# Two-layer streaming encoder on one core: mask copies, the ring of query parts, the quadrant sums, resting outputs and the last residual additions change their places

## The chip, the core and the metric

The kernel runs on one core of a Trainium2 chip. The metric is the device time of one execution in microseconds (us), the median over several runs. A core has five engines that run side by side, each in the order of its own queue: TensorE (PE: matrix products and transposes; the load of its weights is listed as PEld), VectorE (DVE), ScalarE (ACT), GpSimd (POOL) and SyncE (SP), which here only issues transfers. Transfers run on 16 DMA engines. Products are accumulated in banks of PSUM, and everything else lies in SBUF.

## The reference

What is computed are two transformer layers for 1024 prompt frames and 64 sample frames with shared weights, in float32:

```python
xp, xs = x_prompt, x_sample                      # (1, 1024, 1024), (1, 64, 1024)
for l in range(2):
    if l == 0:
        mp = _even_prompt(xp, ...)               # latent attention (8 heads) and chunk-band attention (8 heads)
        ms = _even_sample(xs, ...)
    else:
        mp = _odd_prompt(xp, ...)                # stick-breaking attention, 16 heads
        ms = _odd_sample(xs, ...)
    xp = _post_block(xp, mp, ...)
    xs = _post_block(xs, ms, ...)

def _even_project(x, pos, w_in, g_q, w_uq, g_kv):
    h = x @ w_in
    q_a = (_rms_norm(h[..., :768], g_q) @ w_uq).reshape(B, S, 8, 96)
    q_a = concat([q_a[..., :64], _rope(q_a[..., 64:], pos)])
    ckv = _rms_norm(h[..., 768:1024], g_kv)
    ...

def _post_block(x, mix, g1, b1, g2, b2, w_up, w_down):
    x = _layer_norm(ALPHA * x + mix, g1, b1)
    ff = jnp.square(jax.nn.relu(x @ w_up)) @ w_down      # 1024 -> 4096 -> 1024
    return _layer_norm(ALPHA * x + ff, g2, b2)
```

The outputs are the two results and the new cache rows of each attention.

## The kernel before

All products are done in split precision: a float32 operand is split into a rounded high part H and a remainder L (`split`, L152 on ScalarE and L153 on VectorE), and a product is three matmuls, H by H, H by L and L by H (`mm3`, L157 to L159). So an operand is ready for TensorE only when ScalarE and VectorE have both dealt with it.

The program is written with a tile framework that puts instructions into the queue of each engine in an order that a simulated timeline gives, and adds the waits. A tile's tag names a ring of buffers, and its count is the ring's length: the next tile of a tag waits until the oldest one is no longer read. `after(x, mark)` adds an order without a wait: x is put into its queue only once the instruction `mark` has its place in the timeline. All transfers are issued by SP, in its queue's order, on eight lanes; a transfer waits for the one eight before it.

**Latents and queries (layer 0).** `latents` goes over nine tiles of 128 tokens. First it makes the compressed keys (`cat`, stored to `o_lat`; `stgH`, `stgL` and `krT`, stored to `ck_d` and `krT_d`, L413 to L424). Then it makes the query latents: two products of 384 columns, squares with a sum on ScalarE (L445), a reciprocal root, the scaled `qn` on VectorE (L453), and its transposes on TensorE (L175), which are split into `qn0`, `qn384` and `qn768`. In this second loop, two copies of a constant mask `qconst` into the DRAM tensor `qr_d` are issued (L437), and two of the query weights are loaded and split (`weight`, L193).

`queries` multiplies the latents by six blocks of `w_uq`. Blocks 0 to 3 (`u0` to `u3`) are loaded and split there. Each result is split into H and L in a buffer `raw` (`parts`, L152 and L153) from which it is stored to `qm_d`, or for the rotated blocks by quarters to `qr_d` (L513). TensorE writes the products by turns into banks s and d.

**After the mixer, in both layers.** `out_proj` makes the output projection tile by tile, with a residual (L1186), the layer norm (statistics L296 and L298, `rv` L201, `neg` L302, on ScalarE L303, the scaling L304, the bias L305 on VectorE or GpSimd) and the transposes of the result (L175, from `xs` or `sl`), which are written to the four quadrants of each half c of the tokens. `quadrant_sums(c)` gives a list of closures that are called one by one: four that split a quadrant, then `sums` (four differences on VectorE, L271), then four that split the sums and the last quadrant. `up` multiplies by `w_up`: `plain(m, c)` does the first two blocks of columns in the plain way, `work(m)` does blocks 2 to 15 by a Strassen scheme with seven products that use the sums. The squared outputs go to the DRAM tensor `a_d` (`store`, L1305).

`down` multiplies by `w_down`. `strassen(q)` is called for q = 0 to 48, seven products for each of seven groups; each loads operands three products ahead (`load_a`, L1412; `load_w`), splits them one ahead (`ahead`) and adds the product to accumulators (L1488 on VectorE, L1492 on ScalarE for the first ones). In the last group the combined sums M1, U2 and W1 are added to each other, on GpSimd and VectorE (L1398, the helper `tt`). `finish` does the last group in the plain way: a product for each half of a row tile, added to `acc` (also `tt`, L1398), with W1 and the residual x22 added by L1599 and S0 by `tt`, and then the layer norm.

Big buffers come from a list of free slots (`Slots`): `take` gives the first free one that fits, `give` puts one at the end of the list. The slots are named `sl`, `xs`, `wo`, `wH`, `wL` and `wraw`; a slot that has been given back can be taken at once, and then its next writer waits until a transfer from it is done.

Of the kernel before, what the change touches and what calls it, by code (L numbers as in the profile page):

```python
# [13 lines left out]
P = 128  # L14
# [109 lines left out]
class Net:  # L124
# [116 lines left out]
    def quadrant_sums(self, c):  # L241

        sl = self.slots
        f = dict(enumerate(self.xq[c]))

        def sums():
            f.update({i: sl.take([4, TC]) for i in (4, 5, 6)})
            self.sums(*(f[i] for i in range(7)))  # L250
            for i in (0, 2, 3):
                sl.give(f[i])

        def part(i, give=False):
            if i in self.xqH[c]:
                sl.give(self.xqH[c][i])
                sl.give(self.xqL[c][i])
            H, L = (sl.take([4, TC], F32R) for _ in "HL")
            self.split(H, L, f[i])
            self.xqH[c][i], self.xqL[c][i] = H, L  # L260
            if give:
                sl.give(f[i])

        return [lambda i=i: part(i) for i in (0, 2, 1, 3)] + [sums] + [lambda i=i: part(i, True) for i in (5, 6, 4, 1)]
# [64 lines left out]
    def latents(self):  # L329
# [102 lines left out]
        for t, (t0, n) in enumerate(TOK):  # L432
            if t == 1:

                rows = io["qconst"].unsqueeze(0).to_broadcast([4, ROPE, 2, T])
                for r in (96, 0):
                    self.after(nc.sync.dma_start(self.qr_d[:, r : r + ROPE], rows), marks[-2])  # L437
# [29 lines left out]
    def queries(self, qn, uw):  # L467
# [4 lines left out]
        def load(m):  # L472
            if m < 4:
                raw = self.tl(up, [P, KQ, P], "uraw", 2)
                nc.sync.dma_start(raw, io["w_uq"][m])
                uw[m] = [self.tl(up, [P, KQ, P], f"u{m}{x}", 1, F32R) for x in "HL"]
                self.split(*uw[m], raw, mark=marks[-1])
# [4 lines left out]
        def nope(m, c):  # L482
            c0, n = CHUNKS[c]
            ps = self.ps("ds")
            uq(ps, m, c, n)
            nc.sync.dma_start(self.qm_d[m, :, :, c0 : c0 + n], self.parts(up, ps[:, :n], 4))

        def rotate(c):
# [21 lines left out]
            for i, r in enumerate((x1, x2)):  # L510
                x = self.parts(up, r, 4)
                for o, base in ((0, 64), (1, 32)):
                    nc.sync.dma_start(self.qr_d[:, base + 16 * i : base + 16 * i + 16, :, c0 : c0 + n], x[o * 64 : o * 64 + 64])  # L513
# [748 lines left out]
    def up(self, layer):  # L1262
# [6 lines left out]
        F, W = {}, {}  # L1269
        AHEAD, PLAIN = 3, 2  # L1270

        def load(m):
# [21 lines left out]
        def product(ps, w, XH, XL, first=True, last=True):  # L1294
            for k in range(4):
                self.mm3(ps, w[:, 0, k, :], w[:, 1, k, :], XH[:, k, :], XL[:, k, :], first and k == 0, last and k == 3)

        def store(m, c, out, A):
            s = slice(c * TC, c * TC + TC)
            if m < 14:  # L1300
# [3 lines left out]
                nc.sync.dma_start(self.a_d[m, 4:, :, s].rearrange("i p t -> p i t"), out[1])  # L1304
            nc.sync.dma_start(self.a_d[m, :4, :, s].rearrange("i p t -> p i t"), out[0])  # L1305
            for x in out:
                sl.give(x)

        def plain(m, c):

            out, A = outputs()
            XH, XL = self.xqH[c], self.xqL[c]
            for h in range(2):
                for half in range(2):
                    ps = self.bank()[:, :TC]
                    for j in range(2):
                        b = 2 * j + half
                        product(ps, W[m, 2 * h + j], XH[b], XL[b], j == 0, j == 1)
                    o = A[2 * half + h]
                    nc.scalar.activation(o, ps, AF.Relu)  # L1320
                    nc.scalar.activation(o, o, AF.Square)
                if c:
                    for j in range(2):
                        sl.give(W.pop((m, 2 * h + j)))
            store(m, c, out, A)

        def work(m, hook):
# [57 lines left out]
    def down(self, layer, xres, xout, last):  # L1385
# [9 lines left out]
        prods = ((0, 0), (1, 2), (5, 5), (6, 6), (3, 1), (4, 4), (2, 3))  # L1395
        NQ = 7 * (NG - 1)
        B, A8, A, W = {}, {}, {}, {}
        tt = lambda e, x, y: e.tensor_tensor(x, x, y, op=ALU.add)  # L1398
# [95 lines left out]
        def strassen(q):  # L1494
            gr, m = divmod(q, 7)
            f0, end = gr == 0, gr == NG - 2
            if not end:
                if m == 1:
# [20 lines left out]
            for i in range(4):  # L1519
# [7 lines left out]
                if end:  # L1527
# [10 lines left out]
                    elif m == 5:  # L1538
                        tt(p, U2[i], W1[i])
                        tt(p, W1[i], acc[i + 4][:, hi])  # L1540
                    elif m == 6:
                        tt(nc.vector, acc[i][:, hi], U2[i])
            if m in (0, 1, 5):
# [14 lines left out]
        def finish():  # L1558
# [19 lines left out]
            for t in order:  # L1578
                n = sum(r[1] for r in rows[t])
                for h in range(2):  # L1580
# [3 lines left out]
                    if n == P:  # L1584
                        r = slice(t % 4 * P, t % 4 * P + P)
                        for k in range(4):
                            aH, aL = la[2 * (t // 4) + k // 2]
                            self.mm3(ps, aH[:, k % 2, r], aL[:, k % 2, r], *mov[k], k == 0, k == 3)
                    else:
                        self.mm2(ps, [a8[:, k, :] for k in range(4)], mov)  # L1590
                    tt(nc.vector, acc[t][:, c], ps)
                    if n < P:
# [3 lines left out]
                        sl.give(tmp)  # L1596
                if t == order[0]:
                    for i in range(4):
                        nc.vector.scalar_tensor_tensor(acc[i + 4][:, hi], x22[0][i], ALPHA, W1[i], op0=ALU.mult, op1=ALU.add)  # L1599
                    for c in (lo, hi):  # L1600
                        tt(nc.vector, acc[8][:, c], S0)
                    if not last:
# [56 lines left out]
    def post(self, layer, ws, ys, side, xres, xmid, xout, last):  # L1659
# [36 lines left out]
        do(1, 4)  # L1696
        do(0, 2)
        plain(1, 0)
        load(2)
# [126 lines left out]
```

## Time and profile before

| | before |
|---|---|
| median of 3 runs | 2820.95 us (2818.41 to 2821.55) |
| the profiled execution | 2826.57 us, span 2824.8 us |
| mean granted clock of TensorE | 0.989 |
| busy: PE, PEld | 97%, 89% |
| busy: DVE, ACT, POOL | 76%, 54%, 27% |
| transfers | 331 MB, 117 GB/s |

The span runs from the first to the last instruction of one profiled execution; what lies around it is 1.8 us here. A list of waits names the waiting engine and line, what it waited for, the total in us, how often, and the longest. A row of a timeline has the start in us, the length, engine, line, operation and tiles, and in brackets the idle time before it with what ended it. A row of windows has the stretch, its length, for each of the five engines the busy time and the number of instructions, the granted clock (1.00 is full), the busy share of the DMA engines and GB/s. Buffer numbers are left out of names.

### The profile page before, as it was taken

How to read it: one execution, taken by the hardware profiler on the slowest of the kernel's cores; microseconds unless marked ns; L12 is line 12 of the kernel's file. 1: busy time of each engine (PE TensorE's matmuls, PEld its weight loads, DVE VectorE, ACT ScalarE, POOL GpSimd, SP SyncE). 2: the span in 40 equal slices, each digit the busy share in tenths (PEclk: the TensorE clock that was granted, in tenths of full speed). 3: DMA queues.
4: the chain of work that ended last, by engine and by line, in shares of the span. 5: the costliest groups of instructions: out<-in, count | busy, mean ns of one | idle time of the engine just before them, and what ended most of it. 6: DMA issues, size and time to landing. Idle time of an engine off the chain costs nothing. (4 is left out here: it accounts for less than half of the span.)

```text
span 2824.8 us, 46956 instructions
## 1 busy us (share of the span) xinstructions
PE 2737.9 (97%) x16931; PEld 2500.8 (89%) x16931; DVE 2158.5 (76%) x3833; ACT 1513.2 (54%) x3103; POOL 749.5 (27%) x879
## 2 busy tenths in 40 slices
PE   8999998999999999999999999999999999999998
PEld 7999997888899998788789999998789999977786
DVE  4346667885867777899977888878787777789998
ACT  4236666883555556333257777777545555543331
POOL 3022323652100002222543333434330000022245
PEclk9999999989999999999999999999999999999999
DMA  7142224434244457443421111112252443664432
GB/s 220 36 154 69 67 84 101 109 102 137 88 136 144 134 167 254 127 151 116 134 83 61 52 59 52 54 51 77 79 167 87 153 148 129 227 196 127 151 124 83
DMA packets 226800, 331.33 MB, mean 117 GB/s; under 512 B 44488, under 2 KB 159240, under 8 KB 226504
## 3 DMA queue, kind: packets, MB, share of 16 engines
q1 hardware_dynamic: 226568, 328.34, 36.8%
q8 instruction: 134, 2.20, 0.3%
q14 instruction: 98, 0.80, 0.1%
HBM read 216.58 MB, written 109.99 MB: 116 GB/s over the span
## 5 line engine op out<-in xcount | busy, mean ns | idle before, releaser
L723 POOL TENSOR_TENSOR G<-G,S 128x384 f32<-128x384 f32 (+4 forms) x200 | 200.6, 1007 | 346.3 <-DVE S L720 129.8
L157 PE MATMUL d<-xH,wH 128*128 128x384 f32 (+1 forms) x784 | 262.7, 335 | 3.1 <-ACT qS L608 2.3
L159 PE MATMUL d<-xH,wL 128*128 128x384 f32 (+1 forms) x784 | 261.6, 334 | 0.0
L158 PE MATMUL d<-xL,wH 128*128 128x384 f32 (+1 forms) x784 | 260.4, 332 | 0.0
L153 DVE TENSOR_TENSOR wtL<-t,wtH 128x512 fp32r<-128x512 f32 (+2 forms) x328 | 197.0, 618 | 47.1 <-ACT wtH L152 38.4
L152 ACT ACTIVATE wtH<-t 128x512 fp32r<-128x512 f32 (+2 forms) x328 | 170.3, 545 | 48.1 <-PE t L175 21.4
L1483 POOL MEMSET sl<- 64x1024 f32 x2 | 1.9, 953 | 655.4 <-PE pv L159 328.8
L787 PE MATMUL pv<-wtH,V 128*128 128x256 f32 (+1 forms) x624 | 159.0, 280 | 4.2 <-ACT o L747 2.1
L662 POOL TENSOR_TENSOR R<-R,inv 128x640 f32<-128x640 f32 (+6 forms) x100 | 115.5, 1167 | 177.4 <-DVE inv L661 73.2
L789 PE MATMUL pv<-wtL,V 128*128 128x256 f32 (+1 forms) x624 | 154.0, 288 | 7.7 <-DVE wtL L153 7.6
L157 PEld LDWEIGHTS d<-xH,wH 128*128 128x128 f32 x784 | 148.1, 189 | 7.1 <-ACT qS L608 3.2
L720 DVE TENSOR_TENSOR_SCAN S<-S,own 128x513 f32<-128x513 f32 (+3 forms) x144 | 144.2, 1011 | 11.8 <-ACT S L713 9.9
L158 PEld LDWEIGHTS d<-xL,wH 128*128 128x128 f32 x784 | 148.0, 189 | 1.3
L159 PEld LDWEIGHTS d<-xH,wL 128*128 128x128 f32 x784 | 148.0, 189 | 1.2
L152 ACT ACTIVATE wo<-wo 128x1024 fp32r<-128x1024 f32 (+4 forms) x91 | 81.8, 908 | 123.4 <-PE d L158 28.1
L789 PEld LDWEIGHTS pv<-wtL,V 128*128 128x128 f32 x624 | 120.1, 192 | 11.8 <-DVE wtL L153 10.2
L787 PEld LDWEIGHTS pv<-wtH,V 128*128 128x128 f32 x624 | 120.0, 192 | 9.4 <-ACT o L747 5.1
L175 PE MATMUL t<-ident,G 128*128 128x128 f32 x600 | 104.0, 278 | 14.0 <-POOL S L711 7.2
L655 PE MATMUL s<-kS,qH 128*128 128x384 f32 (+3 forms) x288 | 106.0, 370 | 3.1 <-DVE mx L678 2.1
L713 ACT ACTIVATE S<-s 128x384 f32<-128x384 f32 (+4 forms) x200 | 98.9, 494 | 15.7 <-PE s L655 13.8
L203 POOL TENSOR_TENSOR rr<-rv,mhalf 128x1 f32<-128x1 f32 (+1 forms) x54 | 39.6, 736 | 229.5 <-DVE neg L302 141.1
L714 ACT ACTIVATE G<-s 128x384 f32<-128x384 f32 (+4 forms) x200 | 99.7, 499 | 0.1
(1841 smaller groups left out, 9976.4 us busy)
## 6 DMA issues: line engine op xcount, KB each, us to landing
wo<-a_d SPq DMA_DIRECT2D x54, 512.0 KB
a_d<-wo SPq DMA_DIRECT2D x32, 544.0 KB
wo<-in_w_dn SPq DMA_DIRECT2D x27, 512.0 KB
sl<-a_d SPq DMA_DIRECT2D x24, 512.0 KB
wo<-in_w_up SPq DMA_DIRECT2D x21, 512.0 KB
a_d<-sl SPq DMA_DIRECT2D x19, 544.0 KB
sl<-in_w_up SPq DMA_DIRECT2D x17, 512.0 KB
xs<-a_d SPq DMA_DIRECT2D x17, 512.0 KB
```

Source lines behind the costliest of these rows:

```text
L152: self.after(self.nc.scalar.activation(H, src, AF.Copy), mark)
L153: (engine or self.nc.vector).tensor_tensor(L, src, H.bitcast(F32), op=ALU.subtract)
L157: i = mm(out, aH, bH, start=first, stop=False)
L158: mm(out, aH, bL, start=False, stop=False)
L159: mm(out, aL, bH, start=False, stop=last)
L175: return self.nc.tensor.transpose(out, in_, self.ident[:n, :n])
L655: self.nc.tensor.matmul(ps[:, :n], q, k, start=i == 0, stop=i == len(passes) - 1)
L662: nc.gpsimd.tensor_tensor(R[:, :nk], R[:, :nk], inv.to_broadcast([P, nk]), op=ALU.mult)
L720: nc.vector.tensor_tensor_scan(s[r], s[r], own, carry, op0=ALU.mult, op1=ALU.max)
L723: nc.gpsimd.tensor_tensor(G[:, :n], G[:, :n], S[:, 1 : n + 1], op=ALU.mult)
L787: mm(out, v, wH[:, s : s + n], start=bi == 0 and s == 0, stop=False)
L789: mm(out, v, wL[:, s - n : s], start=False, stop=bi == len(banks) - 1 and j == bank[-1][0])
```

## The change

1. In the second loop of `latents` the two mask copies are asked for at the fifth tile (`t == 4`), not at the second.
2. In `queries` the ring of `raw` has eight buffers, not four; the H and L parts of the four `u` weights share a ring of two each, where each weight had a buffer of its own.
3. In `post`, the sums of half 0 are no longer called before `plain(1, 0)` but after it, with the first product of `plain(1, 0)` as their mark; the split that followed them in the call comes after too.
4. In `store`, the output slots of block 15 are not given back at once but kept in `resting` and given back when `strassen` starts with q = 2.
5. In the last group of `strassen` the addition of U2 to the right half of the first four row tiles is taken out of m == 6 and put into `finish`, behind the first row tile; it and the additions of W1, x22 and S0 that stood there get the last product of that tile as their mark.

```diff
@@ quadrant_sums
-        def sums():
+        def sums(mark=None):
             f.update({i: sl.take([4, TC]) for i in (4, 5, 6)})
-            self.sums(*(f[i] for i in range(7)))
+            self.sums(*(f[i] for i in range(7)), mark=mark)
@@ latents
-            if t == 1:
+            if t == 4:
                 rows = io["qconst"].unsqueeze(0).to_broadcast([4, ROPE, 2, T])
                 for r in (96, 0):
@@ queries
-                uw[m] = [self.tl(up, [P, KQ, P], f"u{m}{x}", 1, F32R) for x in "HL"]
+                uw[m] = [self.tl(up, [P, KQ, P], f"u{x}", 2, F32R) for x in "HL"]
...
-            nc.sync.dma_start(self.qm_d[m, :, :, c0 : c0 + n], self.parts(up, ps[:, :n], 4))
+            nc.sync.dma_start(self.qm_d[m, :, :, c0 : c0 + n], self.parts(up, ps[:, :n], 8))
...
-                x = self.parts(up, r, 4)
+                x = self.parts(up, r, 8)
@@ up
+        self.resting = []
...
             nc.sync.dma_start(self.a_d[m, :4, :, s].rearrange("i p t -> p i t"), out[0])
+            if m == 15:
+                self.resting += out
+                return
             for x in out:
                 sl.give(x)
@@ down, strassen
+        REST = 2
...
+            if q == REST:
+                for x in self.resting:
+                    sl.give(x)
...
-                    elif m == 6:
-                        tt(nc.vector, acc[i][:, hi], U2[i])
@@ down, finish
                 if t == order[0]:
+                    late = [tt(nc.vector, acc[i][:, hi], U2[i]) for i in range(4)]
                     for i in range(4):
-                        nc.vector.scalar_tensor_tensor(acc[i + 4][:, hi], x22[0][i], ALPHA, W1[i], op0=ALU.mult, op1=ALU.add)
-                    for c in (lo, hi):
-                        tt(nc.vector, acc[8][:, c], S0)
+                        late.append(nc.vector.scalar_tensor_tensor(acc[i + 4][:, hi], x22[0][i], ALPHA, W1[i], op0=ALU.mult, op1=ALU.add))
+                    late += [tt(nc.vector, acc[8][:, c], S0) for c in (lo, hi)]
+                    for i in late:
+                        self.after(i, mark)
@@ post
         do(1, 4)
-        do(0, 2)
-        plain(1, 0)
+        mark = plain(1, 0)
+        prep[0].pop(0)(mark)
+        do(0, 1)
```

With ten more lines above them, L1488 of before is L1498 of the changed kernel, L1398 is L1408 and L1599 is L1612.

Three places show how the queues change. The first is SP's queue around the mask copies. `stg` and `krT` are the last stores of the key loop, and `wraw` are the weights of the third and the fifth tile. Before:

```order
L424 DMA krT_d<-krT_666 32x128
L413 DMA o_lat<-cat_703 64x288
L437 DMA qr_d<-in_qconst 4x8x8704
L421 DMA ck_d<-stgH_717 256x1x64
L421 DMA ck_d<-stgL_718 256x1x64
L424 DMA krT_d<-krT_723 32x64
L193 DMA wraw_892<-in_w_uq 128x768
L193 DMA wraw_1050<-in_w_uq 128x768
```

And after the change:

```order
L424 DMA krT_d<-krT_666 32x128
L413 DMA o_lat<-cat_703 64x288
L421 DMA ck_d<-stgH_717 256x1x64
L421 DMA ck_d<-stgL_718 256x1x64
L424 DMA krT_d<-krT_723 32x64
L193 DMA wraw_890<-in_w_uq 128x768
L437 DMA qr_d<-in_qconst 4x8x8704 x2
L193 DMA wraw_1050<-in_w_uq 128x768
```

Both copies now stand behind the stores and the first weight, next to each other, and ahead of the second weight; the first of them stood five rows above this piece before.

The second is VectorE's queue in the layer norm of the last two tiles of layer 0's output projection (`xs_11` and `xs_13` are these tiles, L271 the quadrant sums). Before:

```order
L271 TENSOR_TENSOR wo_0_2283_9440<-sl_6_2146_8633,xs_12_2282_9439 128x1088
L296 BN_STATS st_9252<-xs_11_2196_8898 128x6
L1186 SCALAR_TENSOR_TENSOR xs_13_2207_8987<-xs_13_2207_8987,pv_9104 128x512
L271 TENSOR_TENSOR wo_1_2284_9441<-sl_6_2146_8633,sl_4_2144_8631 128x1088
L296 BN_STATS st_9281<-xs_13_2207_8987 128x6
L276 TENSOR_TENSOR wraw_9568<-wL_2294_9567 128x512
L298 BN_AGGR mv_9255<-st_9252 128x2
L153 TENSOR_TENSOR wo_17_2286_9447<-wo_0_2283_9440,sl_0_2285_9446 128x1088
L296 BN_STATS st_9281<-xs_13_2207_8987 128x6
L271 TENSOR_TENSOR sl_4_2144_8631<-sl_5_2145_8632,wo_0_2283_9440 128x1088
L278 TENSOR_TENSOR wraw_9568<-wraw_9568,wL_2293_9566 128x512
L201 TENSOR_SCALAR rv_9257<-mv_9255 128x1
```

And after the change:

```order
L1186 SCALAR_TENSOR_TENSOR xs_13_2207_8987<-xs_13_2207_8987,pv_9104 128x512
L296 BN_STATS st_9281<-xs_13_2207_8987 128x6
L298 BN_AGGR mv_9255<-st_9252 128x2
L296 BN_STATS st_9281<-xs_13_2207_8987 128x6
L201 TENSOR_SCALAR rv_9257<-mv_9255 128x1
L302 TENSOR_SCALAR neg_9251<-mv_9255 128x1
L276 TENSOR_TENSOR wraw_9568<-wL_2294_9567 128x512
L298 BN_AGGR mv_9284<-st_9281 128x2
L278 TENSOR_TENSOR wraw_9568<-wraw_9568,wL_2293_9566 128x512
L201 TENSOR_SCALAR rv_9286<-mv_9284 128x1
L302 TENSOR_SCALAR neg_9280<-mv_9284 128x1
L304 SCALAR_TENSOR_TENSOR xs_11_2196_8898<-xs_11_2196_8898,rr_9259,wH_2152_8642 128x1024
```

The four sums and the split L153 of a sum have left the piece, and the scaling L304 of both tiles follows right behind their statistics.

The third is VectorE's queue at the end of layer 1's last Strassen group (L1488 adds a product from a bank `pv`, `d`, `t` or `s` to an accumulator). Before:

```order
L153 TENSOR_TENSOR sl_6_6051_31309<-sl_6_6051_31309,sl_4_6054_31315 128x1024
L1488 TENSOR_TENSOR sl_7_5568_28929<-sl_7_5568_28929,pv_31227 128x512
L1599 SCALAR_TENSOR_TENSOR wo_13_5572_28933<-sl_18_6033_31268,wo_8_5565_28926 128x512
L1488 TENSOR_TENSOR sl_2_5569_28930<-sl_2_5569_28930,d_31236 128x512
L1398 TENSOR_TENSOR sl_7_5568_28929<-sl_7_5568_28929,wo_19_5563_28924 128x512
L1488 TENSOR_TENSOR sl_17_5570_28931<-sl_17_5570_28931,t_31245 128x512
L1599 SCALAR_TENSOR_TENSOR sl_8_5573_28934<-sl_18_6033_31268,wo_8_5565_28926 128x512
L1398 TENSOR_TENSOR sl_2_5569_28930<-sl_2_5569_28930,wo_19_5563_28924 128x512
L1488 TENSOR_TENSOR wo_12_5571_28932<-wo_12_5571_28932,s_31254 128x512
L1398 TENSOR_TENSOR sl_17_5570_28931<-sl_17_5570_28931,sl_0_5564_28925 128x512
```

And after the change:

```order
L153 TENSOR_TENSOR wo_14_6051_31305<-wo_14_6051_31305,sl_3_6054_31311 128x1024
L1498 TENSOR_TENSOR sl_7_5568_28929<-sl_7_5568_28929,pv_31227 128x512
L1498 TENSOR_TENSOR sl_2_5569_28930<-sl_2_5569_28930,d_31235 128x512
L1498 TENSOR_TENSOR sl_17_5570_28931<-sl_17_5570_28931,t_31243 128x512
L1408 TENSOR_TENSOR sl_2_5569_28930<-sl_2_5569_28930,wo_19_5563_28924 128x512
L1612 SCALAR_TENSOR_TENSOR wo_13_5572_28933<-sl_11_6033_31264,wo_3_5565_28926 128x512
L1612 SCALAR_TENSOR_TENSOR sl_8_5573_28934<-sl_11_6033_31264,wo_3_5565_28926 128x512
L1408 TENSOR_TENSOR sl_1_5576_28937<-sl_1_5576_28937,sl_5_5567_28928 128x512
L1408 TENSOR_TENSOR sl_17_5570_28931<-sl_17_5570_28931,sl_0_5564_28925 128x512
L1498 TENSOR_TENSOR wo_12_5571_28932<-wo_12_5571_28932,s_31251 128x512
```

The reader of bank `t` has moved ahead of the residual additions, and the reader of bank `s` stands behind five of them, not four.

More of the change, by code (lines that the diff above doesn't have):

```diff
@@ L1295, in product @@
             for k in range(4):
-                self.mm3(ps, w[:, 0, k, :], w[:, 1, k, :], XH[:, k, :], XL[:, k, :], first and k == 0, last and k == 3)
+                i = self.mm3(ps, w[:, 0, k, :], w[:, 1, k, :], XH[:, k, :], XL[:, k, :], first and k == 0, last and k == 3)
+            return i
         def store(m, c, out, A):
@@ L1312, in plain @@
             XH, XL = self.xqH[c], self.xqL[c]
+            mark = None
             for h in range(2):
@@ L1317, in plain @@
                         b = 2 * j + half
-                        product(ps, W[m, 2 * h + j], XH[b], XL[b], j == 0, j == 1)
+                        i = product(ps, W[m, 2 * h + j], XH[b], XL[b], j == 0, j == 1)
+                        mark = mark or i
                     o = A[2 * half + h]
@@ L1325, in plain @@
             store(m, c, out, A)
+            return mark
         def work(m, hook):
@@ L1587, in finish @@
                             aH, aL = la[2 * (t // 4) + k // 2]
-                            self.mm3(ps, aH[:, k % 2, r], aL[:, k % 2, r], *mov[k], k == 0, k == 3)
+                            mark = self.mm3(ps, aH[:, k % 2, r], aL[:, k % 2, r], *mov[k], k == 0, k == 3)
                     else:
```

## The prediction

> **What bounds the kernel now.** I read the page's busy shares first, then the list of TensorE's waits, then the windows around each wait for the granted clock, and last the rows of the engine that each wait names.
>
> ```profile
> span 2824.8 us, 46956 instructions
> PE 2737.9 (97%) x16931; PEld 2500.8 (89%) x16931; DVE 2158.5 (76%) x3833; ACT 1513.2 (54%) x3103; POOL 749.5 (27%) x879
> ```
>
> TensorE is busy for 97% of the span, so the products set the end. The change takes no product away. It can only gain where TensorE stands still, 2824.8 - 2737.9 = 87 us in all, or where it runs at a lower clock. The list of TensorE's waits (total, times, longest) names the places; these are the rows that the change can touch:
>
> ```profile
> PE t L175 <- DVE qn L453: 9.4, 2, 7.2
> PE s L157 <- DVE raw L153: 3.1, 2, 2.7
> PE t L175 <- DVE sl L305: 2.2, 2, 1.9
> PE s L157 <- DVE wo L1488: 2.0, 1, 2.0
> PE s L157 <- DVE wo L1398: 1.9, 1, 1.9
> PE t L175 <- DVE xs L305: 1.8, 1, 1.8
> PE t L158 <- DVE wL L153: 1.4, 1, 1.4
> PE t L157 <- ACT wo L152: 1.2, 1, 1.2
> PE d L157 <- DVE raw L153: 1.0, 1, 1.0
> ```
>
> They add up to 24.0 us. A wait can cost more than itself. In the windows (stretch, length, busy time of each engine, then the granted clock) each row is the stretch of work behind one of these waits:
>
> ```profile
> 64.60:68.20 3.60, 3.54 (x14) 3.55 (x15) 1.56 (x3) 0.98 (x2) 0.00 (x0) 0.51 0.52 197
> 78.00:82.00 4.00, 3.95 (x16) 3.94 (x17) 1.55 (x3) 0.98 (x2) 0.00 (x0) 0.57 0.17 65
> 762.30:766.30 4.00, 3.93 (x33) 3.72 (x34) 2.67 (x4) 3.40 (x5) 0.00 (x0) 1.00 0.68 266
> 2133.20:2137.50 4.30, 4.26 (x23) 4.29 (x24) 4.30 (x5) 3.68 (x5) 0.00 (x0) 0.60 0.33 126
> 2771.50:2776.00 4.50, 4.42 (x13) 3.53 (x14) 4.50 (x8) 0.00 (x0) 0.55 (x1) 0.62 0.00 0
> ```
>
> Behind four waits TensorE got 0.51 to 0.62 of its clock for about 4 us, which loses 3.6 x 0.49 = 1.8, 4.0 x 0.43 = 1.7, 4.3 x 0.40 = 1.7 and 4.5 x 0.38 = 1.7 us. Behind the wait at 760 us it kept 1.00. So a wait of about 2 us is followed by a loss of 1.7 us in some cases and by none in others.
>
> **The change part by part.** *The mask copies.* Two copies of qconst to DRAM were issued here, ahead of the last stores of the latents and of tile 2's weight:
>
> ```profile
> 47.78 0.77 SPq L437 DMA_DIRECT2D qr_d<-in_qconst  x1
> 52.45 0.69 SPq L437 DMA_DIRECT2D qr_d<-in_qconst  x1
> 61.42 0.54 SPq L421 DMA_DIRECT2D ck_d<-stgH  x1
> 61.85 0.29 DVE L153 TENSOR_TENSOR stgL<-t,stgH 128x128 fp32r<-128x128 f32 x1 [12.47 <-DMA ck_d<-stgL]
> 74.53 0.84 ACT L152 ACTIVATE wH<-wraw 128x768 fp32r<-128x768 f32 x1 [7.82 <-DMA wraw<-in_w_uq]
> ```
>
> SP stands before the store at 61.42 until the first copy is done, so that copy takes 61.4 - 47.8 = 13.6 us. VectorE sits 12.47 us behind it with the first qn work queued there, and TensorE waits 7.2 us for it. The weight, issued at 63.40, is used at 74.53, behind the second copy; that is the other 2.2 us. After, the weight is ahead of both copies, so neither wait has its cause any more: 9.4 us, and 1.8 + 1.7 us of lost clock, 12.9 us. What comes late next is tile 4's weight, which stands behind both copies. With no wait before them they issue at about 54 (52.45 plus three short issues). Two at 11 to 13.6 us each, one behind the other, end at 76 to 81. The weight's two uses were here:
>
> ```profile
> L152 ACT ACTIVATE wH<-wraw x2: 845/846/847, 74.5 to 89.8; 128x768 fp32r<-128x768 f32 x2
> 98.33 1.00 ACT L152 ACTIVATE qn384H<-t 128x384 fp32r<-128x384 f32 x2 [1.47 <-PE t L175]
> ```
>
> It now stands one square later in ScalarE's queue, between 89.8 and the qn split of 98.33 and nearer to the latter; I put it at 95, which is 95 - 13 = 82 in the new time. The margin is 1 to 6 us. Between a loss of 12.9 kept in full and nothing lost again I take a gain of 12.4.
>
> [...]
>
> *The ring of eight, two tags for the u weights.* ScalarE waited before the split of each product because a part's buffer was still being stored:
>
> ```profile
> 160.70 0.49 ACT L152 ACTIVATE raw<-s 128x384 fp32r<-128x384 f32 x1 [7.26 <-DMA qr_d<-raw]
> ...
> 168.61 0.44 ACT L152 ACTIVATE raw<-s 128x320 fp32r<-128x320 f32 x1 [3.46 <-DMA qr_d<-raw]
> ```
>
> TensorE's share is 3.1 + 1.0 = 4.1 us. Eight buffers let the first eight parts go without a wait. Four of the later ones still wait for a store, but for one issued eight parts earlier, not four. The u weights now share two buffers, so the third u is split after the first one's last product. Between lie five products of 18 matmuls; at 0.15 us (row 161.60 below: 18 in 2.9 us) that is 14 us of cover for a split of the shape whose ScalarE half took 0.85 (the wH rows above). Bounds: 0 (the stores set the pace anyway) and 4.1; I take 3.6, near the upper end since the last two waits in ScalarE were hidden but for 1.0 us.
>
> ```profile
> 161.60:165.60 4.00, 2.91 (x18) 2.65 (x18) 0.60 (x2) 0.49 (x1) 0.00 (x0) 1.00 0.27 100
> ```
>
> *The quadrant sums.* In layer 0 VectorE does four sums and a split in between the statistics of the last two tiles:
>
> ```profile
> 742.70 1.29 DVE L271 TENSOR_TENSOR xs<-sl,sl 128x1088 f32<-128x1088 f32 x1 [5.00 <-PE pv L159]
> 751.20 1.24 DVE L153 TENSOR_TENSOR wo<-wo,sl 128x1088 fp32r<-128x1088 f32 x1
> 752.96 1.27 DVE L271 TENSOR_TENSOR sl<-sl,wo 128x1088 f32<-128x1088 f32 x1
> 755.46 0.15 DVE L201 TENSOR_SCALAR rv<-mv 128x1 f32<-128x1 f32 x1
> 758.47 2.48 DVE L304 SCALAR_TENSOR_TENSOR xs<-xs,rr,wH 128x1024 f32<-128x1024 f32 x2 [0.83 <-ACT xs L303]
> 760.87 2.35 DVE L305 TENSOR_TENSOR xs<-xs,xs 128x1024 f32<-128x1024 f32 x2
> 740.00:760.00 20.00, 20.00 (x142) 19.00 (x141) 15.76 (x25) 8.14 (x13) 1.22 (x2) 1.00 0.17 53
> ```
>
> Without them the second rv comes 3 to 4 sums and a split earlier, 4.8 to 6 us, so 749.5 to 750.7; the scaling comes 3.0 later, as now, and the first L305 ends 3.6 us after that starts, at 756.1 to 757.3. TensorE's transposes move 27 matmuls forward, 27 x 0.14 = 3.8 us, and want the tile at 756.3 to 757. So between 0 and 1 us of the 1.8 remains. In layer 1 the order changes in the same way, and the transposes of its last tile keep their place, so its 2.2 us go, with the 1.7 us of lost clock behind them. The sums, 4 x 1.2 us in a layer, go behind this; there VectorE has room, by this row of layer 1 it is idle for 11 of 34 us:
>
> ```profile
> 2136.00:2170.00 34.00, 34.00 (x271) 34.00 (x270) 23.06 (x30) 18.81 (x36) 0.00 (x0) 0.99 0.26 88
> ```
>
> If that room did not serve, the sums' 4.8 us would show as a wait in each layer. Bounds -9.6 and +5.7; I take 5.0.
>
> *The resting outputs.* Two slots of the last squared outputs are given back at the third Strassen product, not at once, so that no early split takes a slot whose store is under way. In layer 0 this was the row:
>
> ```profile
> 1111.07 1.06 ACT L152 ACTIVATE wo<-xs 128x1024 fp32r<-128x1024 f32 x1 [1.25 <-DMA a_d<-wo]
> 1112.00:1116.50 4.50, 2.89 (x11) 2.10 (x12) 4.34 (x3) 4.50 (x8) 1.65 (x1) 1.00 0.99 327
> ```
>
> TensorE's two waits there are 1.2 + 1.4 = 2.6 us, and the second follows from ScalarE being late. The DMA share of 0.99 is the reason not to take it all: the loads for the same products are near their limit too. Bounds 0 and 2.6; I take 2.0.
>
> *The last residual additions.* Four additions in each layer move behind the last part's first product. VectorE has no room there:
>
> ```profile
> 2700.00:2800.00 100.00, 97.98 (x416) 77.60 (x415) 96.62 (x130) 27.50 (x27) 51.24 (x29) 0.98 0.29 97
> 2766.37 1.18 DVE L1398 TENSOR_TENSOR sl<-sl,wo 128x512 f32<-128x512 f32 x1
> 2769.17 1.76 DVE L1398 TENSOR_TENSOR sl<-sl,wo 128x512 f32<-128x512 f32 x1
> 2770.85 0.67 DVE L1488 TENSOR_TENSOR wo<-wo,s 128x512 f32<-128x512 f32 x1
> ```
>
> In layer 1 TensorE waits for the last of these rows, which frees bank s. Before it the queue held two residual additions and two scalings; after, it holds two additions, two scalings and one sum of S0. Each op of two SBUF tensors takes 1.2 to 1.8 us while GpSimd works, so the bank comes about 0.8 us later. In layer 0 one op fewer stands before the bank's reader, 0.7 us gained. Together 0; bounds -3 (one more op, and the clock's 1.7) and +3.9 (both waits gone).
>
> [...]
>
> Sum: 12.4 + 3.6 + 5.0 + 2.0 + 0 = 23.0 us. The profiled execution took 2826.57 us, 1.8 beyond its span; less 23.0 that is 2803.6. The runs' median is 2820.95, 5.6 less than the profiled one, so the forecast for the median is **2798 us**.
>
> **The rivals.**
>
> *The waits only move.* The copies end at 81 or later and tile 4's weight takes half of the first gain back (6 us), the stores' pace keeps the 3.6 us, and one layer's sums stand in the way (2.5): 23 - 12 = 11 us, 2810. For it: the copies are still 25 us of transfer ahead of a weight. Against it: the order leaves only one of these in each place, and the margins above cover them.
>
> *It does not do what it says.* The copies hold tile 4's weight for a whole copy's 13 us and the sums, queued late, cost their 4.8 in both layers: 23 - 12 - 9.6 = 1 us left, 2819.5. Against: both would have to miss their margins in full.
>
> *Two slots missing at the start of Strassen, slower.* The resting slots are held through two products in each layer. The loads run three products ahead; a product is 48 matmuls at 97.98 / 416 = 0.236, 11.3 us. If the missing slots put loads back so far that a whole product is waited for, it costs 11.3 us each time; with two of them, one in each layer, the gain of 23 is gone, and from the third on the kernel is slower: 2798 + 34 = 2832. Against: it must overcome a lead of 34 us, and the two slots are held for 23.
>
> **How the numbers follow.** Chances: forecast 0.70, the waits only move 0.20, no gain 0.06, slower 0.04. About 0.2% (5.6 us) is what this kernel's timing can tell from no change. Faster is then 0.90, same 0.06, slower 0.04. The forecast's own range takes the bounds: all terms at their upper end, 12.9 + 4.1 + 5.7 + 2.6 + 3.9 = 29 us, give 2792, and 16 us 2805. The range reaches to the first rival and a little past both ends, 2790 to 2811.
>
> **What would show it.** The two waits of t for qn at L453 are gone and the clock stays at 1.00 from 57 to 82 us; the use of tile 4's weight has no idle time put down to its load. ScalarE's raw rows have no idle time over 1 us on a store of qr_d. The waits of t for L305 fall from 4.0 to below 1 us. ScalarE's split at about 1111 no longer waits for a_d. The waits of s on the residual lines stay near 4 us in sum. I am wrong if TensorE waits anew between 75 and 90 us, or if its total of waits falls by less than 12 us.

## The result and the profile after

The changed kernel's median is 2799.69 us (2797.94 to 2800.94, 4 runs) beside 2821.25 us for the kernel before (2818.41 to 2827.53, 4 runs): 21.6 us less, a ratio of 0.992 with a 95% interval of 0.9902 to 0.9938. The forecast was 2798.

The head of the page of the changed kernel, and from its list of TensorE's waits the rows that answer to those shown of before:

```profile
span 2796.1 us, 46947 instructions
PE 2724.9 (97%) x16931; PEld 2491.2 (89%) x16931; DVE 2160.2 (77%) x3833; ACT 1511.9 (54%) x3103; POOL 749.5 (27%) x879
...
PE s L157 <- DVE wo L1498: 3.4, 1, 3.4
...
PE s L157 <- DVE wo L1408: 1.2, 1, 1.2
...
PE d L157 <- DVE raw L153: 1.0, 1, 1.0
```

The span of the profiled executions fell by 28.7 us. TensorE's idle time fell from 86.9 to 71.2 us, and its busy time from 2737.9 to 2724.9 us with the same 16,931 matmuls. So 15.7 us are waits that are gone, and 13.0 us are matmuls that had taken longer at a low clock (mean granted clock 0.989 before, 0.994 after). Only some 5 of these 13 us lie where something was changed: four stretches of low clock that cost 1.7 us each stood there before, and one stands there after. The rest lies where nothing was changed and differs from one execution to the next: in a second trace of the changed kernel (mean granted clock 0.993) TensorE is busy for 2729.4 us, 4.5 more. So these two executions lie further apart than the medians; the one of before is near the slow end of its runs, and the one of after is the fastest of its four.

Of the nine rows of before, 24.0 us in sum, three rows with 5.6 us stand in the list of after, 18.4 us less; the idle time fell by only 15.7, so about 2.7 us turned up as waits elsewhere. The waits for qn (9.4 us), for L305 (4.0 us in both layers) and at 1111 us for the weights and outputs (2.6 us) are gone. The three for raw in the query products (4.1 us) are gone too; the 1.0 us in the row of after is a new wait, behind them, in the first products of the next stage:

```profile
181.42 0.44 PE L157 MATMUL d<-xH,wH 128*128 128x384 f32 x1 [1.04 <-DVE raw L153]
```

There ScalarE had waited 10.75 us for the weights `w_bq`, whose load SP issued behind four stores of the query parts, and the splits of the last raw parts stood behind that. The two waits for bank s at the end of each layer went from 3.9 to 4.6 us: 1.2 in layer 0, 3.4 in layer 1.

SP's queue around the mask copies, and ScalarE's second split of a query weight (start, length, engine, line):

```profile
54.53 0.41 SPq L193 DMA_DIRECT2D wraw<-in_w_uq  x1
54.99 1.49 SPq L437 DMA_DIRECT2D qr_d<-in_qconst  x2
61.17 0.37 SPq L193 DMA_DIRECT2D wraw<-in_w_uq  x1
...
80.26 0.83 ACT L152 ACTIVATE wH<-wraw 128x768 fp32r<-128x768 f32 x1
```

The copies were issued at 55 us, as forecast (54). The weight behind them, issued at 61.17, was used at 80.26 without any idle time. The windows of this stretch show when the copies were done:

```profile
66.00:72.00 6.00, 6.00 (x38) 5.95 (x37) 1.38 (x4) 1.98 (x6) 0.25 (x1) 1.00 0.27 116
72.00:78.00 6.00, 6.00 (x39) 5.96 (x38) 1.88 (x4) 1.46 (x4) 0.30 (x1) 1.00 0.25 107
78.00:84.00 6.00, 6.00 (x36) 6.00 (x35) 2.61 (x6) 1.31 (x3) 0.55 (x1) 1.00 0.04 16
78.00:80.00 2.00, 2.00 (x13) 2.00 (x12) 0.28 (x1) 0.22 (x1) 0.00 (x0) 1.00 0.12 49
```

TensorE is busy throughout at a clock of 1.00. The DMA share stands at about 0.25, as much as four engines of sixteen, until 78. What follows, 2 us at 49 GB/s, is 98 KB, which is four sixteenths of the weight's 393 KB (128 x 768 float32): by this sum the two copies took 23 us, to 78, and the weight's share on their four engines moved only behind them. That traffic ends between 79.5 and 79.75 us, about 0.5 us before the weight's use.

In the layer norm of layer 0, L305 of the last two tiles (timeline of VectorE) now runs before TensorE wants it, and in layer 1 the same stretch is full:

```profile
733.93 1.22 DVE L305 TENSOR_TENSOR xs<-xs,xs 128x1024 f32<-128x1024 f32 x1
735.42 1.22 DVE L305 TENSOR_TENSOR xs<-xs,xs 128x1024 f32<-128x1024 f32 x1
2085.00:2110.00 25.00, 25.00 (x187) 24.17 (x186) 23.18 (x33) 13.16 (x20) 2.07 (x2) 1.00 0.24 86
```

At the end of layer 1 the queue of VectorE ahead of the reader of bank s is this, with the windows of the wait and of what follows:

```profile
2735.25 1.25 DVE L1408 TENSOR_TENSOR sl<-sl,wo 128x512 f32<-128x512 f32 x1
2736.42 1.77 DVE L1612 SCALAR_TENSOR_TENSOR wo<-sl,wo 128x512 f32<-128x512 f32 x1
2738.12 1.77 DVE L1612 SCALAR_TENSOR_TENSOR sl<-sl,wo 128x512 f32<-128x512 f32 x1
2739.82 2.35 DVE L1408 TENSOR_TENSOR sl<-sl,sl 128x512 f32<-128x512 f32 x2
2742.09 0.67 DVE L1498 TENSOR_TENSOR wo<-wo,s 128x512 f32<-128x512 f32 x1
2739.00:2743.00 4.00, 0.62 (x3) 0.20 (x3) 4.00 (x5) 0.00 (x0) 2.01 (x2) 1.00 0.00 0
2743.00:2748.00 5.00, 5.00 (x16) 3.88 (x16) 4.96 (x9) 0.00 (x0) 0.00 (x0) 0.66 0.00 0
```

Five additions with two inputs in SBUF, 1.2 to 1.8 us each, run without a gap ahead of the reader, and behind the wait TensorE has 0.66 of its clock for 5 us, 1.7 us lost.

### The profile page after: what moved, and what is told of

Same layout as the page of the kernel before. It is cut to its first block, busy times and chain, and to the rows that moved or that the text cites. A ratio compares the mean times of both kernels' runs of the same rounds, so it can differ in the third digit from the quotient of the medians.

```text
span 2796.1 us, 46947 instructions
## 1 busy us (share of the span) xinstructions
PE 2724.9 (97%) x16931; PEld 2491.2 (89%) x16931; DVE 2160.2 (77%) x3833; ACT 1511.9 (54%) x3103; POOL 749.5 (27%) x879
## 5 line engine op out<-in xcount | busy, mean ns | idle before, releaser
L153 DVE TENSOR_TENSOR wtL<-t,wtH 128x512 fp32r<-128x512 f32 (+2 forms) x328 | 196.9, 618 | 45.5 <-ACT wtH L152 36.7
L175 PE MATMUL t<-ident,G 128*128 128x128 f32 x600 | 103.3, 277 | 14.6 <-POOL S L711 7.8
L655 PE MATMUL s<-kS,qL 128*128 128x384 f32 (+3 forms) x288 | 97.0, 339 | 0.0
```

Source lines behind the costliest of these rows:

```text
L153: (engine or self.nc.vector).tensor_tensor(L, src, H.bitcast(F32), op=ALU.subtract)
L175: return self.nc.tensor.transpose(out, in_, self.ident[:n, :n])
L655: self.nc.tensor.matmul(ps[:, :n], q, k, start=i == 0, stop=i == len(passes) - 1)
```

## The experiments

My theory was the prediction's: each part removes the wait that its row names, with the lost clock behind it, and the last part is worth nothing. The rival was that waits only move, so that undoing one part costs much less than its term. Five kernels each undo one part of the change, and the others test a cause or change the last part. Each was run five times or so beside the kernel before; the interval of each ratio is about 0.0013 to either side, 3.7 us, so differences of 2 to 5 us between two of these kernels rest on the waits in their traces as much as on the times. Where two kernels ran on different chips, only their ratios can be set against each other, and such a difference is uncertain by some 5 us to either side (1.4 x 3.7).

### The changed kernel again

> The changed kernel once more, beside the others on this chip: 2800 us, ratio to the kernel before 0.992. It is the zero for the differences of this set, and its spread is theirs.

Measured: 2801.82 us (2800.55 to 2802.26) beside 2823.01 for the kernel before, ratio 0.9923 (0.9909 to 0.9936). This is the zero for the next three.

### The mask copies at the second tile

```diff
-            if t == 4:
+            if t == 1:
```

> The changed kernel with the mask copies asked for at the second tile again, all else kept. My theory: both waits of TensorE for qn and the low clock behind them come back, 12.4 us in the profile as the prediction had it, about 2812 us (ratio to the kernel before 0.9965). Rival (the waits only moved, and other parts made up the gain): 4 to 6 us, about 2805. Rival (only the bare waits count, the clock's loss turns up elsewhere anyway): 9.4 us, 2809.

Measured: 2814.14 us (2812.29 to 2817.61), ratio 0.9968 (0.9956 to 0.998), 12.3 us more than the changed kernel; the theory's 12.4 holds and both rivals fall. From the list of waits, and the windows behind the two waits:

```profile
PE t L175 <- DVE qn L453: 9.0, 2, 7.3
...
64.50:71.50 7.00, 5.03 (x19) 5.04 (x20) 2.57 (x6) 1.73 (x6) 0.55 (x1) 0.52 0.46 158
...
80.00:84.00 4.00, 4.00 (x26) 3.95 (x26) 1.40 (x4) 1.56 (x4) 0.00 (x0) 1.00 0.16 65
```

The first wait is again followed by half the clock, which costs 5.03 x 0.48 = 2.4 us of TensorE's work; the second one (1.7 us here) is not. In this execution the lost clock is one stretch, not two, and 9.0 + 2.4 = 11.4 of the 12.3 us are seen.

### The same place, with the rows as the slowest dimension

```diff
-            if t == 4:
-                rows = io["qconst"].unsqueeze(0).to_broadcast([4, ROPE, 2, T])
+            if t == 1:
+                rows = io["qconst"].unsqueeze(1).to_broadcast([ROPE, 4, 2, T])
...
-                    self.after(nc.sync.dma_start(self.qr_d[:, r : r + ROPE], rows), marks[-2])
+                    self.after(nc.sync.dma_start(self.qr_d[:, r : r + ROPE].rearrange("m r x t -> r m x t"), rows), marks[-2])
```

> As u1_masks_t1, with the copies at the second tile, but the 32 rows of the mask are the slowest dimension of each transfer and the four copies the second one. The bytes and the place in SP's queue are the same. Theory (a copy was slow because its slowest dimension of 4 put it on four DMA engines): the copies spread, each is done in about 3 us (1088 KB at the 300 GB/s and more that the windows of before reach at best), no wait for qn is left, and the time is that of the changed kernel, 2800 us. Rival (the bytes, or their place ahead of the stores, are what delays): the waits for qn stay at 9 us and the time is that of u1_masks_t1.

Measured: 2802.56 us (2800.01 to 2805.33), ratio 0.9926 (0.9914 to 0.9939), the time of the changed kernel within what can be told, with the copies at their old place. The wait, and the windows after the first copy's issue at 50.5:

```profile
PE t L175 <- DVE qn L453: 1.0, 1, 1.0
...
53.00:57.00 4.00, 4.00 (x24) 4.00 (x23) 0.00 (x0) 0.00 (x0) 0.00 (x0) 1.00 0.97 311
57.00:61.00 4.00, 3.02 (x19) 2.73 (x18) 1.56 (x5) 1.26 (x5) 0.55 (x1) 1.00 1.04 350
61.00:65.00 4.00, 3.99 (x25) 3.79 (x24) 1.28 (x3) 1.29 (x3) 0.00 (x0) 1.00 0.37 123
```

With the same bytes from the same place in SP's queue the DMA share is 0.97 to 1.04 from 53 to 61 us, where the kernel with 4 as the slowest dimension has 0.48 (53 to 57) and 0.24 (57 to 61). Both copies, issued at 50.5 and 55.1, are by these windows through at about 62, within 12 us of the first issue; those of the changed kernel took 23 us by the sum above, 11.5 each. So it was neither the bytes nor the place that delayed the stores, but the order of the dimensions: with 4 as the slowest one the share falls to between 0.24 and 0.27 while the copies are under way, with 32 it stands at 0.97 to 1.04.

### The ring of four and a buffer for each u weight

```diff
-                uw[m] = [self.tl(up, [P, KQ, P], f"u{x}", 2, F32R) for x in "HL"]
+                uw[m] = [self.tl(up, [P, KQ, P], f"u{m}{x}", 1, F32R) for x in "HL"]
...
-            nc.sync.dma_start(self.qm_d[m, :, :, c0 : c0 + n], self.parts(up, ps[:, :n], 8))
+            nc.sync.dma_start(self.qm_d[m, :, :, c0 : c0 + n], self.parts(up, ps[:, :n], 4))
...
-                x = self.parts(up, r, 8)
+                x = self.parts(up, r, 4)
```

> The changed kernel with the ring of four for the query parts and a buffer of its own for each u weight. Theory: TensorE waits for raw again, 4.1 us in the list of waits against 1.0 in the changed kernel, and the time is 3 to 4 us longer, 2803 us. Rival (the stores' pace is the bound, so the ring moves the waits only): within 1 us of the changed kernel.

Measured: 2807.19 us (2804.36 to 2808.78), ratio 0.9941 (0.9928 to 0.9953), 5.4 us more. In its list of waits

```profile
PE s L157 <- DVE raw L153: 3.2, 2, 2.8
...
PE d L157 <- DVE raw L153: 1.0, 1, 1.0
```

are back in the query products, 4.2 us, where the changed kernel has none; its wait of 1.0 us for raw at 181 us, in the next stage, isn't in this trace. So 3.2 us net of the 5.4 are waits, and the rest isn't settled (the ranges allow 2 us less). The ring and the shared buffers of the u weights were undone together; what each does alone isn't shown. That the ring only moves the waits is refuted for TensorE: of 4.2 us it moves 1.0. For ScalarE it is half true: in the changed kernel it still waits for these stores, later and shorter.

```profile
156.32 0.49 ACT L152 ACTIVATE raw<-s 128x384 fp32r<-128x384 f32 x1 [3.07 <-DMA qr_d<-raw]
158.32 0.85 ACT L152 ACTIVATE uH<-uraw 128x768 fp32r<-128x768 f32 x1 [1.50 <-DMA qr_d<-raw]
160.37 0.44 ACT L152 ACTIVATE raw<-d 128x320 fp32r<-128x320 f32 x1 [1.21 <-DMA qr_d<-raw]
```

### The quadrant sums ahead of the plain product

```diff
-        mark = plain(1, 0)
-        prep[0].pop(0)(mark)
-        do(0, 1)
+        do(0, 2)
+        plain(1, 0)
```

> The changed kernel with the quadrant sums called before the plain product again. Theory: the waits of t for L305 come back in both layers, 4.0 us, and layer 1's is again followed by a stretch of low clock in some executions, 0 or 1.7 us: 4 to 6 us slower than the changed kernel, 2804 to 2806. Rival (the sums cost the same wherever they stand): within 1 us.

Measured: 2810.1 us (2803.46 to 2811.41) beside 2825.1 for the kernel before on this chip, ratio 0.9944 (0.993 to 0.9958), which is 0.0021 or 6 us above the changed kernel's. The waits come back to the tenth, and the one of layer 1 is followed by a low clock:

```profile
PE t L175 <- DVE sl L305: 2.2, 2, 1.9
...
PE t L175 <- DVE xs L305: 1.8, 1, 1.8
2113.50:2118.00 4.50, 4.46 (x24) 4.50 (x25) 4.50 (x5) 3.90 (x5) 0.00 (x0) 0.62 0.31 120
```

4.0 and 4.5 x 0.38 = 1.7 make 5.7 us. They carry this verdict: the 6 us are a difference between two chips and uncertain by as much as 5.

### The outputs given back at once

```diff
-            if m == 15:
-                self.resting += out
-                return
```

> The changed kernel with the output slots of block 15 given back at once. Theory: in layer 0 ScalarE waits again for a store of a_d and TensorE 2.6 us for it, so 2 to 3 us slower, 2802 us. Rival (the DMA engines near their limit set the pace there, and the slot's wait hid in theirs): within 1 us.

Measured: 2807.9 us (2806.24 to 2811.1), ratio 0.994 (0.9928 to 0.9953), 4.8 us above the changed kernel by the ratios. In layer 0's first Strassen products, where the changed kernel has no wait in this list:

```profile
PE t L158 <- DVE wL L153: 1.6, 1, 1.6
PE t L157 <- ACT wo L152: 1.2, 1, 1.2
1095.00:1099.00 4.00, 3.73 (x10) 3.00 (x11) 4.00 (x6) 3.08 (x5) 0.00 (x0) 0.58 0.71 195
```

These are 2.8 us, and behind them TensorE lost 3.73 x 0.42 = 1.6 us to a low clock, which the trace of before doesn't have at this place (1.00 in its row at 1112). Another 0.8 us is a wait of s that is 2.0 there and 1.2 in the changed kernel, perhaps because the slots of the whole of `down` are dealt out otherwise; that isn't shown. The rival, that the DMA engines set the pace, is refuted by the waits that came back. The 4.8 us, between two chips, don't say more than that the part is worth a few us.

### The last residual additions as before

```diff
+                    elif m == 6:
+                        tt(nc.vector, acc[i][:, hi], U2[i])
...
-                    late = [tt(nc.vector, acc[i][:, hi], U2[i]) for i in range(4)]
...
-                    for i in late:
-                        self.after(i, mark)
```

> The changed kernel with the U2 additions in the last Strassen group and no marks in finish, as before. Theory (one op more ahead of the reader of bank s in layer 1, one fewer in layer 0): the two waits of s go back from 1.2 and 3.4 us to 1.9 and 2.0, so the sum falls by 0.7 us, and the time is 0 to 1 us shorter than that of the changed kernel, 2799. Rival (the late additions help, the longer wait of layer 1 is chance): 1 to 3 us slower.

Measured: 2798.44 us (2795.73 to 2800.97), ratio 0.9906 (0.9893 to 0.992): 4.8 us *below* the changed kernel by the ratios, uncertain by some 5 us. The rival falls, and the theory had the sign right; whether its 0 to 1 us was too small the times alone don't tell. In layer 1 a wait of s of 1.5 us is left, with the full clock behind it:

```profile
PE s L157 <- DVE wo L1498: 1.5, 1, 1.5
2747.00:2752.00 5.00, 5.00 (x22) 4.09 (x23) 4.97 (x8) 0.00 (x0) 0.34 (x1) 1.00 0.00 0
```

In layer 0 no wait of s is left, but another one has grown. About 25 us ahead of that place TensorE waits for a split on VectorE, 0.5 us in the changed kernel and 1.9 here, and here a low clock follows:

```profile
PE t L158 <- DVE sl L153: 1.9, 1, 1.9
1361.00:1366.00 5.00, 4.86 (x14) 3.88 (x15) 5.00 (x9) 3.90 (x4) 1.24 (x1) 0.66 0.06 21
```

So in layer 0 the wait has moved (1.2 + 0.5 us against 1.9), and what the traces show as gained lies in layer 1: 1.9 us of wait, and the 1.7 us of clock behind it. There the last part of the change made the kernel slower. It does two things, and two runs part them.

### The marks alone, and the move alone

The first of these keeps the marks on the W1, x22 and S0 additions and puts the U2 additions back into the Strassen group; the second keeps the move and drops the marks. The edit of the second is:

```diff
-                    for i in late:
-                        self.after(i, mark)
```

> The changed kernel with the U2 additions back in the last Strassen group, but the marks on the W1, x22 and S0 additions kept. Undoing the whole of part 5 made the kernel about 4 us faster; this tells which half does it. If the marks cost (they gather the additions into one run ahead of the reader of bank s, so that none fills VectorE's earlier waits for GpSimd): time as the changed kernel, wait of s for L1498 near 3.4 us. If the moved U2 additions cost: time and waits as with part 5 undone, 2798 us.

> The other half: the U2 additions in finish, but none of the additions has a mark. If the marks cost: as with part 5 undone, 2798 us and a wait of s of about 1.5 us. If the move costs: as the changed kernel, 2801 us.

Measured: marks alone 2800.71 us (2798.77 to 2802.49), ratio 0.9915 (0.9902 to 0.9929); the move without marks 2798.03 us (2792.97 to 2799.99), ratio 0.9903 (0.989 to 0.9917). The times alone don't part them (the intervals overlap). The waits do, in layer 1 (L1498); the L1408 row and the row of bank t are layer 0's, and the windows stand behind layer 1's wait. With marks alone:

```profile
PE s L157 <- DVE wo L1498: 3.3, 1, 3.3
PE s L157 <- DVE wo L1408: 1.8, 1, 1.8
PE t L158 <- DVE sl L153: 0.6, 1, 0.6
2748.00:2753.00 5.00, 5.00 (x16) 3.95 (x15) 5.00 (x9) 0.00 (x0) 0.00 (x0) 0.66 0.00 0
```

and without marks:

```profile
PE s L157 <- DVE wo L1498: 1.7, 1, 1.7
PE t L158 <- DVE sl L153: 1.9, 1, 1.9
2745.00:2750.00 5.00, 5.00 (x23) 4.05 (x22) 4.97 (x8) 0.00 (x0) 0.17 (x1) 1.00 0.01 3
```

In layer 1 the wait is 3.3 against 1.7 us. With the marks and the move (the changed kernel) it is 3.4, with neither 1.5, so it is the marks and not the move. The low clock goes with it: in all eight traces with the marks in layer 1's `finish` the wait is 3.3 to 3.5 us, and the windows behind it show 0.62 to 0.66 of the clock in four of them (both traces of the changed kernel, the outputs given back at once, the marks alone); in the three without marks there it is 1.5 to 1.7 us, with the clock at 1.00. In layer 0 the waits of s and t make 2.4 us with marks alone and 1.9 without marks, 1.7 in the changed kernel and 1.9 with neither, so there the marks only say where TensorE waits. How the queues differ fits: without a mark an addition slips between the readers of earlier banks, with one all of them stand in a row ahead of the reader of bank s.

### Each addition behind its own row tile

In layer 1 the U2, W1 and S0 additions were spread over the products of `finish`, so that none stands ahead of the readers of banks t and s.

```diff
+                own = {8: (), order[1]: (order[1], 8)}.get(t, (t,)) if last else range(9) if t == order[0] else ()
+                for i in own:
...
```

> The changed kernel with, in layer 1 only, each of the last residual additions behind the product of its own row tile, not all of them behind the first one; in VectorE's queue the reader of bank s then stands right behind that of bank t, with no addition between. Theory: the wait of s for L1498 (3.4 us) and the low clock behind it (5.0 x 0.34 = 1.7 us) vanish, and the additions find room beside the plain products: 3 to 5 us shorter, 2795 to 2797. Rival (VectorE is so full to the end, 97%, that the additions only come late in the tail): the same time, with the wait moved to later products or to the time behind TensorE's last product (8.66 us now).

> As x5_own_tile (that one, by the place of its W1 and x22 additions, wrote over the products of the right half of row tiles 4 to 7 in layer 1, with the same instructions), with these additions one tile earlier. x5_own_tile had no wait of s in layer 1, but 14.0 us behind TensorE's last product against 8.65, and the changed kernel's time. If the tail is what VectorE's load moves to: the same again, 2801 us. If it came from the order of the last tile alone: a tail near 9 us and about 2797.

Measured: 2801.72 us (2800.8 to 2804.75, ratio 0.992) and, with the W1 additions a tile earlier so that nothing is written over, 2803.16 us (2800.36 to 2805.18, ratio 0.9924, 0.9911 to 0.9936). No wait of s is left in layer 1 in either, and nothing is gained. The last matmul of the changed kernel and of the second of these, and the second one's last 40 us:

```profile
2787.07 0.40 PE L159 MATMUL d<-wo,wo 128*128 128x512 f32 x1
```

```profile
2784.03 0.40 PE L159 MATMUL d<-wo,wo 128*128 128x512 f32 x1
2760.00:2799.80 39.80, 24.43 (x105) 19.35 (x104) 35.69 (x56) 6.91 (x6) 21.28 (x14) 0.87 0.26 99
```

TensorE is done 3 us earlier, but the program ends 15.4 us after that (2799.8 less 2784.4), not 8.6 us (2796.1 less 2787.5). VectorE is busy for 35.7 of these 39.8 us, and an addition that leaves the queue ahead of bank s is met again in the tail. The rival was right.

### Parts 1 to 4 with spread copies

> Parts 1 to 4 of the change without part 5, and the mask copies at the fifth tile with their 32 rows as the slowest dimension. Expected: the time of part 5 undone, 2797 us, since no wait stands behind the copies any more at the fifth tile, and a lead over the changed kernel of 3 to 5 us. If the spread copies delay other transfers there, TensorE's waits between 75 and 90 us show it.

Measured: 2799.85 us (2798.59 to 2802.0), ratio 0.9913 (0.99 to 0.9927). The lead over the changed kernel that I expected can't be told from nothing, and spreading copies behind which nothing waits gained nothing that can be seen. Apart from the copies this is the kernel with part 5 undone; its lead by the ratios is 2.8 us here and was 4.8 there, which shows how far such a figure can be trusted. The best of all was the changed kernel without the marks, 2798.03 us, and its interval (0.989 to 0.9917) still overlaps that of the changed kernel (0.9902 to 0.9938 in the first set).

## Why the prediction was right

The time (2798 forecast, 2799.7 measured) came from a sum of terms. Measured by undoing each part, the terms are as follows; the last three are ratios between chips, uncertain by some 5 us each:

| term | forecast | undone, by the times | waits in the trace |
|---|---|---|---|
| mask copies | 12.4 | 12.3 | 9.0 and 2.4 of clock |
| ring of eight | 3.6 | 5.4 | 4.2, less 1.0 in the next stage |
| quadrant sums | 5.0 | 6 | 4.0 and 1.7 of clock |
| resting outputs | 2.0 | 4.8 | 2.8 and 0.8, and 1.6 of clock |
| residual additions | 0 | -4.8 | -3.1 and +1.4; clock -1.7 in layer 1, +1.6 in layer 0 |
| sum | 23.0 | 23.7 | |

- **The mask copies.** Right in size and in mechanism. The copies ended at 78, within the forecast 76 to 81. The margin of 1 to 6 us was reckoned from their end to the weight's use and left out that, by the sum above, the weight's own share on the same four engines comes behind them: 2.3 us lay between, and about 1.7 of them went to that share, so some 0.5 us was left. That nothing was lost again was closer than forecast. That the lost clock counts was the step that mattered, since the waits alone would have given 9.4.
- **The ring.** Right for TensorE; I had taken off 0.5 us for waits that remain. None remains in the query products, and one of 1.0 us came up in the next stage. The sign named for ScalarE did not come: two of its raw rows still wait 3.07 and 1.21 us for stores of qr_d, and TensorE doesn't wait for them.
- **The quadrant sums.** The residue of 0 to 1 us that I allowed in layer 0 did not come: the first L305 ended at 735.1 us, 2.3 us before its transposes began (the row of L175 below). I had set the scaling (L304) 3.0 us behind the second tile's rv, as before; it came 0.2 us behind that one (730.81) and 2.1 us behind the first tile's rv, whose result it uses. Before, the two rv stood 0.7 us apart, and VectorE waited for ScalarE's L303 between them and the scaling.

```profile
728.87 0.14 DVE L201 TENSOR_SCALAR rv<-mv 128x1 f32<-128x1 f32 x1
731.00 1.28 DVE L304 SCALAR_TENSOR_TENSOR xs<-xs,rr,wH 128x1024 f32<-128x1024 f32 x1
737.41 1.03 PE L175 MATMUL t<-ident,xs 128*128 128x128 f32 x8
```

- **The resting outputs.** Too small: I held back 0.6 us because the DMA share stood at 0.99, and the two waits come back in full when it is undone, 2.8 us. The share was the wrong row to hold back by, since no wait of TensorE for a load took the place of the one for the slot. The low clock behind them, 1.6 us, was in no term, since the trace of before has none there.
- **The residual additions.** The weakest step. "Together 0" counted one op more in layer 1 and one fewer in layer 0, 0.8 us lost and 0.7 gained. Layer 0 came out so (1.9 to 1.2 us of wait for s); in layer 1 the wait grew by 1.4 us, from 2.0 to 3.4. What I did not see is that the comparison with the kernel before was the wrong one. With the other four parts in place and without the marks layer 1 waits 1.5 to 1.7 us at the full clock, so the marks took away a gain that would have been there: 1.7 to 1.9 us of wait and 1.7 us of clock in layer 1, and about nothing in layer 0.

By the times the errors of the last two terms are 2.8 and 4.8 us, with opposite signs, so that the total is closer than its terms; that is luck, as far as these two figures can be trusted.

Of the rivals, "the waits only move" is refuted by the first four undone parts, which cost 12.3, 5.4, 6 and 4.8 us and bring their waits back; it is true for the last part, in the tail of layer 1 and at the end of layer 0, and for the 1.0 us behind the query products. "No gain" and "two slots missing" did not happen: the changed kernel has no wait in the first Strassen products of layer 0.

## What to carry to other kernels

A short wait of TensorE is priced with the clock that it may cost behind it (here 1.7 to 1.8 us behind each of four waits, nothing behind three others), and that loss is read from the granted clock in the windows after the wait, not from the list of waits. A transfer that is late though few bytes move is first looked at for its slowest dimension: here the share stood at 0.25 with a slowest dimension of 4 and at 0.97 to 1.04 with one of 32, and the other order was worth as much as the other place in the queue (2802.6 and 2801.8 us). Where one engine is full to the end, as VectorE was at 97%, the order of its work is worth a look: gathered ahead of a bank's reader it cost a wait of 3.4 us against 1.5 here, and put behind the readers it came back in the tail (15.4 us behind the last product against 8.6). When a wait is gone, the stretch around it is read again: here one of bank s came back 25 us earlier at bank t. The margin of a load behind a slow copy is counted to the end of the load, not of the copy.

## What the runs showed of the hardware

The low clock behind a wait depends on more than the wait's length. Waits of 7.2, 2.2, 1.9 (layer 1) and 2.0 us were followed by some 4 us at 0.51 to 0.62 of the clock, while in the same execution one of 2.7, one of 1.8 and one of 1.9 us (layer 0's last) were not; the second wait for qn was followed by it at 2.2 us before and not at 1.7 us with the copies put back. What these stretches cost hardly varies: 0.49 x 3.6, 0.43 x 4.0, 0.40 x 4.3 and 0.38 x 4.5 us before and 0.34 x 5.0 after are all 1.7 to 1.8 us; with the copies put back it was 2.4. Two waits of 1.9 us in the trace of before went different ways, 0.60 of the clock behind layer 1's and 1.00 behind layer 0's; what decides it isn't shown. One run of the same kernel differs from the next along with the clock: the mean granted clock of the changed kernel's four first runs was 0.992 to 0.994 with times from 2797.9 to 2800.9 us.
